# A two-layer conv/RWKV-7 trunk on one core: the mixer loop's steps, tiles and queues rearranged

## The chip, the core and the metric

The kernel runs on one NeuronCore of a Trainium2 chip. The metric is the device time of one execution, in microseconds (us); the median of several executions is compared. The engines are PE (TensorE: matmuls and transposes), DVE (VectorE), ACT (ScalarE), POOL (GpSimd) and SP (SyncE, which here only issues DMAs). Each engine works through its own queue of instructions in order, and an instruction waits at the head of its queue until what it needs is there.

## The reference

Two layers; each is a half-step SwiGLU feed-forward block, a token mixer and a second feed-forward block, each followed by `layer_norm(alpha * x + sublayer(x))`. There are 16 meta tokens and 512 tokens, 528 rows of 1024 features, all float32. The mixer has two branches, whose sum is gated:

```python
def _mixer(x, w_in, ...):
    z = x @ w_in
    glu_a, glu_b, zr, gate_c, gate_r = jnp.split(z, ...)
    yc = _conv_branch(glu_a, glu_b, ...)   # depthwise, 31 taps, layer norm, silu, @ conv_wo
    yr = _rwkv_branch(zr, ...)             # 16 heads of 64
    h = jax.nn.sigmoid(gate_c) * yc + jax.nn.sigmoid(gate_r) * yr
    return h @ w_out

def step(S, inp):                          # the RWKV-7 recurrence, for each token
    r_t, w_t, k_t, v_t, kk_t, a_t = inp
    sa = jnp.einsum("bhvk,bhk->bhv", S, -kk_t)
    S = (S * w_t[:, :, None, :] + sa[..., None] * (kk_t * a_t)[:, :, None, :]
         + v_t[..., None] * k_t[:, :, None, :])
    y = jnp.einsum("bhvk,bhk->bhv", S, r_t)
    return S, y
```

The heads' outputs are normalised per head, a bonus term is added, and the result is multiplied by a gate and by `rwkv_wo`.

## The kernel before

Every float32 matrix is split into a high part (a cast on ACT, line 124 for weights) and a low part (a subtraction on DVE, line 133), and a product is three matmuls of the parts. Rows are worked in two halves of 264 columns. A large product is thus a series of 128x264 matmuls: line 186 in the feed-forward blocks and at the join, line 204 in the mixer loop.

A layer runs as feed-forward, **mixer loop**, **join** (products with `rwkv_wo`, `conv_wo`, `w_out`), feed-forward. The recurrence is done in a chunked form: 8 chunks of 64 tokens and one of the 16 meta tokens, for 4 "quarters" of 4 heads. For a quarter the loop has these steps:

- `prep`: the projections of keys, values and the like (line 204), norms of the keys by a product with a block matrix `bones` (lines 882, 884), a reciprocal root on DVE (lines 339 to 346), transposes of it (line 894), a bonus product (944), elementwise work.
- `scores`: for each chunk, transposes (993) and products (1002) into PSUM tiles `sc`, two copies on ACT (1008), four masks on DVE (1010, 1012), and a write of the result to DRAM (1014).
- `substitution`: the triangular 16x16 blocks of all 32 matrices, read back from DRAM with blocks on partitions (1056), are inverted by 15 pairs of small DVE instructions (1035, 1039). ACT copies the transposed result (1042), SP writes both to DRAM (1059) and loads them in another layout as `dd` (1063). The meta block has a substitution of its own on four partitions.
- `inverse`: the 16x16 inverses are joined to 64x64 ones by short products (1081, 1092) with DVE masks (1083) and ACT copies (1085, 1096).
- `scan`: the chunks in order; each has short products (1167, 1175, 1177, 1184, 1192) and a state update on DVE (1187, 1188). `scores` of the next quarter is emitted along with it at lower priority.
- `post`: group norm per head (lines 1220 to 1241), transposes (1289), bonus and gate (1293, 1294), and a write of the rows to DRAM (1295). For the last quarter these writes are issued by POOL.

Two kinds of work fill the gaps. The convolution has 8 x 30 **taps** on DVE (line 821, each a 128x528 multiply-add into `cacc`), emitted at the lowest priority, the last 15 of a layer behind the last quarter's group norm. On TensorE, 32 **fill units** of 48 matmuls (line 204: the convolution's inputs and the gates) are emitted where the table `FILL` says.

The order on an engine is set by a scheduler, from the order in which the program emits instructions, their priorities and its own model of their times. A tile in a pool with `bufs=1` is written anew only when its last reader is done. At the join the branch's rows come back from DRAM by SP (line 1355), eight tiles in three fetches, are split on ACT and DVE (99, 100), and the first dense matmul (186) reads them.

Of the kernel before, what the change touches and what calls it, by code (L numbers as in the profile page):

```python
# [41 lines left out]
LOTS = (2, 2, 2, 1)  # L42
LOW = [(j, o) for o in range(8) for j in (0, 2)] + [(1, o) for o in range(8)]
NORMB = "ch"
# [5 lines left out]
CLATE = 16  # L50
# [15 lines left out]
BONB = 1  # L66
# [19 lines left out]
class Trunk:  # L86
# [10 lines left out]
    def split(self, x, hi, lo):  # L97

        self.nc.scalar.copy(hi, x)
        self.nc.vector.tensor_tensor(lo, x, hi.bitcast(F32), op=ALU.subtract)  # L100

    def wunit(self, *srcs, dst=None, dma=False):
# [20 lines left out]
        if self.cuts == 1 or not CUTA:  # L123
            self.nc.scalar.copy(hi[:, :kt], raw[:, :kt])  # L124
# [6 lines left out]
        for i in range(0, kt, n):  # L131
            k = slice(i, i + n)
            self.nc.vector.tensor_tensor(lo[:, k], raw[:, k], hi[:, k].bitcast(F32), op=ALU.subtract)  # L133
# [61 lines left out]
    def mac(self, pm, w, x, t0, n, nk, wk=0, xk=0, first=True, last=True):  # L195
# [4 lines left out]
        for k in range(nk):  # L200
            for j, (a, b) in enumerate(((hi, xh), (hi, xl), (lo, xh))):
                for h in range(2):
                    s = t0 + h * n
                    nc.tensor.matmul(  # L204
                        pm[:, h, :n], a[:, wk + k, :], b[:, xk + k, s:s + n],
                        start=first and k == 0 and j == 0,
                        stop=last and k == nk - 1 and j == 2)


    def setup(self):  # L210
# [49 lines left out]
        self.behind = None  # L260

# [72 lines left out]
    def rsqrt(self, x, np_, n):  # L334
# [6 lines left out]
        for _ in range(3):  # L341
            e = nc.vector if NEWTON else nc.gpsimd
            e.tensor_tensor(t, y, y, op=ALU.mult)
            if NEWTON:
                e.scalar_tensor_tensor(t, t, -0.5, x, op0=ALU.mult, op1=ALU.mult)
                e.scalar_tensor_tensor(y, t, 1.5, y, op0=ALU.add, op1=ALU.mult)
            else:
                e.tensor_tensor(t, t, x, op=ALU.mult)
                e.tensor_scalar(t, t, -0.5, 1.5, op0=ALU.mult, op1=ALU.add)
                e.tensor_tensor(y, y, t, op=ALU.mult)  # L350
# [227 lines left out]
    def mixer(self, l, last, pre, more):  # L578
# [28 lines left out]
        mpool, self.mp = self.enter(f"mix{l}")  # L607
        cpool, self.cvp = self.enter(f"conv{l}")
# [896 lines left out]
```

## Time and profile before

| | us |
|---|---|
| median of 3 executions (3315.62 to 3325.91) | 3321.35 |
| the profiled execution's own time | 3312.69 |
| its span in the profile | 3311.0 |
| feed-forward blocks of both layers: 0 to 428, 1262 to 2077, 2902 to 3311 | 1652 |
| mixer loops: 428 to 1118 and 2077 to 2745 | 1358 |
| joins: 1118 to 1262 and 2745 to 2902 | 301 |

The stages' bounds were read off the first and last instructions of their lines in the trace. A row that groups instructions names the line, the engine, the operation, the tile written and the tiles read, the shapes and the count; then the busy time and the mean of one in ns; then how long the engine stood idle just before these instructions, and what it waited for. A row of waits reads "engine, tile and line that waited <- engine, tile and line waited for: us in total, times, longest". A row in order of time has start and length in us; a number in brackets behind it is the idle time just ahead of it on that engine. PE's granted clock is given as a share of full speed.

### The profile page before, as it was taken

Reading aid. Unit: us, or ns where it says so; the run is one execution under the profiler, and the core shown is the slowest. Engines: PE = TensorE matmul, PEld = TensorE weight load, DVE = VectorE, ACT = ScalarE, POOL = GpSimd, SP = SyncE. Lnnn points to the kernel's source line nnn. Section 1 sums busy time; section 2 is a strip of 40 time slices with the busy share of each in tenths; the row PEclk is TensorE's granted clock in tenths of the full one; section 3 lists DMA queues with packets and bytes.
Section 4 is the critical chain, followed back from the end, with each engine's and each line's share of the span. In section 5 each row is a group of like instructions: output and inputs, shape, how many; then the busy total and the mean of one; then the engine's idle time right before and its main releaser. Section 6 shows DMA issues by size and latency. Waiting matters only on the chain.

```text
span 3311.0 us, 64968 instructions
## 1 busy us (share of the span) xinstructions
PE 3154.2 (95%) x27172; PEld 3028.1 (91%) x27172; DVE 1957.2 (59%) x4171; ACT 1228.9 (37%) x2469; POOL 19.7 (1%) x89
## 2 busy tenths in 40 slices
PE   9999999799999899999999999997999998999998
PEld 8999989689889799999989999896898897999997
DVE  4343478787874876343453435697878648663434
ACT  4232254244444444232242322542444444342322
POOL 0000000000000000000000000000000000000000
PEclk9999999798989899999999999997999898999998
DMA  5232244223323552232232322542323235432321
GB/s 153 72 107 78 82 152 131 60 61 102 96 83 97 159 145 81 81 108 83 79 96 75 111 75 74 171 120 53 82 85 98 83 100 163 137 90 79 108 81 52
DMA packets 569012, 326.48 MB, mean 99 GB/s; under 512 B 83148, under 2 KB 535104, under 8 KB 568718
## 3 DMA queue, kind: packets, MB, share of 16 engines
q1 hardware_dynamic: 563726, 312.74, 32.9%
q10 hardware_dynamic: 4608, 8.52, 0.7%
q8 instruction: 213, 3.49, 0.4%
q0 software_dynamic: 384, 1.07, 0.1%
q14 instruction: 81, 0.66, 0.1%
HBM read 270.81 MB, written 47.12 MB: 96 GB/s over the span
## 4 chain that ended last, share of the span: by engine, by line
PE 85%; DVE 8%; ACT 3%; issue 2%; DMA 2%; SPq 0%; ACTq 0%; DVEq 0%
PE mm L186 52%; PE mm L204 18%; PE sc L1002 2%; DVE cacc L821 1%; PE ch L1192 1%; PE sc L1092 1%; PE tr L1167 1%; PE ch L1184 1%; DVE is L1035 1%; DVE ix L1039 1%; PE tr L1175 1%; DVE w_lo L133 1%; PE sc L757 1%; PE ch L1092 1%; PE ch L882 1%
## 5 line engine op out<-in xcount | busy, mean ns | idle before, releaser
L186 PE MATMUL mm<-xh,w_hi 128*128 128x264 f32 (+1 forms) x2880 | 819.5, 286 | 17.0 <-ACT xh L396 16.3
L186 PE MATMUL mm<-xh,w_lo 128*128 128x264 f32 (+1 forms) x2880 | 821.3, 285 | 0.5 <-DVE w_lo L133 0.5
L186 PE MATMUL mm<-xl,w_hi 128*128 128x264 f32 (+1 forms) x2880 | 819.0, 285 | 0.3 <-DVE xl L397 0.2
L133 DVE TENSOR_TENSOR w_lo<-w_raw,w_hi 128x1024 fp32r<-128x1024 f32 (+3 forms) x524 | 528.4, 1011 | 470.1 <-ACT w_hi L124 388.0
L124 ACT CAST w_hi<-w_raw 128x1024 fp32r<-128x1024 f32 (+2 forms) x396 | 380.7, 963 | 788.1 <-PE mm L186 540.0
L186 PEld LDWEIGHTS mm<-xh,w_hi 128*128 128x128 f32 x2880 | 546.0, 190 | 19.7 <-ACT xh L396 17.9
L186 PEld LDWEIGHTS mm<-xh,w_lo 128*128 128x128 f32 x2880 | 547.6, 190 | 0.8 <-DVE w_lo L133 0.8
L186 PEld LDWEIGHTS mm<-xl,w_hi 128*128 128x128 f32 x2880 | 546.9, 190 | 1.0 <-DVE xl L397 0.9
L204 PE MATMUL mm<-xh,w_hi 128*128 128x264 f32 x1760 | 399.1, 304 | 40.0 <-DVE v L705 16.2
L204 PE MATMUL mm<-xh,w_lo 128*128 128x264 f32 x1760 | 394.2, 302 | 15.7 <-DVE w_lo L133 15.7
L186 PE MATMUL mm<-hl,w_hi 128*128 128x264 f32 (+1 forms) x1408 | 400.5, 284 | 0.0
L186 PE MATMUL mm<-hh,w_hi 128*128 128x264 f32 (+1 forms) x1408 | 400.3, 284 | 0.0
L186 PE MATMUL mm<-hh,w_lo 128*128 128x264 f32 (+1 forms) x1408 | 398.7, 283 | 0.0
L204 PE MATMUL mm<-xl,w_hi 128*128 128x264 f32 x1760 | 397.1, 303 | 0.0
L821 DVE SCALAR_TENSOR_TENSOR cacc<-cu,cw,cacc 128x528 f32<-128x528 f32 (+1 forms) x480 | 362.6, 755 | 25.3 <-ACT cacc L819 17.7
L204 PEld LDWEIGHTS mm<-xh,w_hi 128*128 128x128 f32 x1760 | 294.9, 200 | 49.7 <-issue 22.6
L204 PEld LDWEIGHTS mm<-xh,w_lo 128*128 128x128 f32 x1760 | 293.8, 200 | 22.4 <-DVE w_lo L133 16.6
L204 PEld LDWEIGHTS mm<-xl,w_hi 128*128 128x128 f32 x1760 | 294.1, 200 | 6.6
L444 DVE TENSOR_TENSOR g<-g,mm 128x264 f32<-128x264 f32 (+1 forms) x176 | 74.8, 427 | 334.2 <-PE mm L186 321.7
L186 PEld LDWEIGHTS mm<-hh,w_lo 128*128 128x128 f32 x1408 | 265.1, 188 | 0.1
L186 PEld LDWEIGHTS mm<-hl,w_hi 128*128 128x128 f32 x1408 | 264.9, 188 | 0.2
L186 PEld LDWEIGHTS mm<-hh,w_hi 128*128 128x128 f32 x1408 | 264.6, 188 | 0.1
(333 smaller groups left out, 4471.7 us busy)
## 6 DMA issues: line engine op xcount, KB each, us to landing
w_raw<-in_w_in_dram SPq DMA_DIRECT2D x116, 512.0 KB
w_raw<-in_ffn_wg_dram SPq DMA_DIRECT2D x88, 512.0 KB
w_raw<-in_ffn_wu_dram SPq DMA_DIRECT2D x88, 512.0 KB
w_raw<-in_ffn_wd_dram SPq DMA_DIRECT2D x64, 384.0 KB
w_raw<-in_ffn_wd_dram SPq DMA_DIRECT2D x64, 320.0 KB
w_raw<-in_rwkv_wo_dram SPq DMA_DIRECT2D x16, 512.0 KB
w_raw<-in_conv_wo_dram SPq DMA_DIRECT2D x16, 512.0 KB
w_raw<-in_w_out_dram SPq DMA_DIRECT2D x16, 512.0 KB
```

The lines of the kernel that those rows point to most:

```text
L124: self.nc.scalar.copy(hi[:, :kt], raw[:, :kt])
L133: self.nc.vector.tensor_tensor(lo[:, k], raw[:, k], hi[:, k].bitcast(F32), op=ALU.subtract)
L186: self.nc.tensor.matmul(pm, a[:, k, :], b[:, xk + k, s], start=first and k == 0 and j == 0, stop=last and k == nk - 1 and j == 2)
L204: nc.tensor.matmul(pm[:, h, :n], a[:, wk + k, :], b[:, xk + k, s:s + n], start=first and k == 0 and j == 0, stop=last and k == nk - 1 and ...
L444: nc.vector.tensor_tensor(g, g, ps[1][:, :n], op=ALU.mult)
L757: nc.tensor.matmul(pm, w[a][r, o, :], x[b][r, s], start=j == 0, stop=j == 2)
L821: tap = nc.vector.scalar_tensor_tensor(y, x, w, y, op0=ALU.mult, op1=ALU.add)
L882: nc.tensor.matmul(tr[:, 2 * j:2 * j + 2], sq[:, NM + j * P:NM + (j + 1) * P], self.bones[:, ::HS], start=True, stop=True)
L1002: pairs.append(nc.tensor.matmul(ps[e][:, p * P:(p + 1) * P], FB[p][r, fs], G[r, p, 1, :, cs], start=True, stop=True))
L1035: steps.append(nc.vector.tensor_tensor(yv, M[r, j, j + 1:, None].to_broadcast([n, w, k]), X[r, j, None, 0:k].to_broadcast([n, w, k]), op=A ...
L1039: steps.append(nc.vector.tensor_tensor(xv, xv, yv, op=ALU.add))
L1092: nc.tensor.matmul(ps[0:W, i * w:(i + 1) * w], vt[:, i, :], x[:, NM * b0:C], start=True, stop=True)
```

## The change

The computation is the same. The parts are:

- **Taps** are emitted a few at a time at each step of `prep`, `scores` and `scan`, by the tables `TAP0`, `TAPP` and `TAP`, with a priority little below their neighbours' (`TAP_LATE`), and go into two buffers of `cacc`. All are emitted before the loop ends. The first tap after a reciprocal root or a substitution is ordered behind its last step (`self.hold`).
- **Substitution in halves**: each half of a quarter has four chunks' blocks on 64 partitions; the first half takes the meta block's four matrices along (68 partitions), so that these have no substitution of their own. The first half is emitted after half of the score chunks, the second after all. `inverse` runs in halves too; the second is emitted in the first scan step.
- **Masks in one step**: `sc` is one PSUM tile of two banks instead of two tiles of one. A chunk has two masks instead of four and one copy instead of two; the bonus product and the low-rank products are read out in one instruction as well.
- **32 columns**: the last of the short inverse products are 32 columns wide instead of 16, and those with `bones` 32 instead of 2.
- **Fill units** move: two stand at the fourth score chunk and two at the eighth of the first quarter, two and one in later `prep` steps, three in the last scan, and the last one behind the last transposes of the loop (`LAST`, `self.later`).
- **The branch's rows** are fetched by POOL instead of SP. Tiles of the mixer and the join are reserved in a fixed order (`places`), and the first splits of the join's weights are ordered behind the last split of those rows (`self.first`). The scratch space for DMAs that POOL describes is set to 4096 bytes.

Line numbers shift: 204 becomes 214, 821 becomes 872, 894 becomes 940, 1010 and 1012 become 1050 and 1052, 1035 and 1039 become 1077 and 1080, 1042 becomes 1084, 1081 becomes 1112, 1092 becomes 1121, 1289 becomes 1303, 1295 becomes 1309, 1355 becomes 1370.

```diff
-FILL = ((0, 0, 0, 0, 0, 0), 2, (0, 0, 0, 0, 0, 2), (4, 4, 5, 5), ((0, 0, 0, 0, 0, 1), (0, 0, 0, 0, 0, 0)))
-CONV_LATE = 4000
+FILL0 = (0, 0, 0, 0, 2, 0, 0, 0, 2)
+FILL = ((0, 0, 0, 0, 0, 0, 0, 0), (0, 0, 0, 0, 0, 0, 0, 0), (0, 0, 0, 0, 0, 0, 0, 0), (0, 1, 0, 1, 0, 1, 0, 0))
+FILLS = (3, 3, 4, 2)
+LAST = 1
+SCORES = (2, 1, 1, 1, 1, 1, 1, 1)
+TAP_LATE = 150
...
         for c, _ in enumerate(self.scores(0, Q)):
-            if c == META[0]:
-                self.meta_inverse(0, Q)
+            if c == 4:
+                self.substitution(0, 0, Q)
+            filler(FILL0[c])
+            if c:
+                self.taps(TAP0[2])
+        self.substitution(0, 1, Q)
+        self.inverse(0, 0, Q)
         self.meta(0, Q)
-        self.inverse(0, Q)
-        filler(FILL[1])
...
             for c, _ in enumerate(self.scan(q, Q)):
+                if c == 0:
+                    self.inverse(q, 1, Q)
                 with self.tc.high_priority(offset=-SC_LATE):
-                    next(scores, None)
+                    for _ in range(SCORES[c]):
+                        next(scores, None)
+                        done += 1
+                        if done == 5 and q < 3:
+                            self.substitution(q + 1, 0, N)
...
+                filler(FILL[q][c])
+                self.taps(TAP[q][c])
...
+    def taps(self, n):
+        with self.tc.high_priority(offset=-TAP_LATE):
+            while n > 0 and self.convs:
+                if next(self.convs[0], None) is None:
+                    self.convs.pop(0)
+                else:
+                    n -= 1
...
     def sc(self):
-        return self.pp.tile([P, 512], F32, name="sc", bufs=2)
+        return self.pp.tile([P, 2, 512], F32, name="sc", bufs=1)
...
-            for e in range(2):
-                pv = ps[e][:, 0:2 * P].rearrange("a (p f t) -> a p f t", p=2, f=2)
-                nc.scalar.copy(U.rearrange("a (p e) t -> a p e t", e=2)[:, :, e], pv[C:P, :, 0, :])
...
+            nc.vector.tensor_tensor(SB[:, c, :, 0:C].rearrange("a (p e) t -> a e p t", e=2),
+                                    pv[:, :, :, 1, :], mask[:, 1], op=ALU.mult)
...
-            w = C - NM * b0
-            for (U, d, dt, y, vt), ps in zip(groups, bank):
...
+            c0 = min(NM * b0, C - 2 * NM)
+            for i in range(N):
+                x = dt[:, i] if b0 == 1 else y[:, i // 4, i % 4]
+                nc.tensor.matmul(ps[0:W, i, c0:C], vt[:, i, :], x[:, c0:C],
                                  start=True, stop=True)
...
-            load = nc.sync.dma_start(out=h[:, a:b, s], in_=yrv[:, a:b, s])
+            load = nc.gpsimd.dma_start(out=h[:, a:b, s], in_=yrv[:, a:b, s])
```

What the scheduler makes of this is seen in the order on the engines. First DVE in the first quarter, where the substitution of quarter 0 begins (`is`, `ix`: its steps; `cacc`: taps; `sb`, `G <- sc, msk`: masks of score chunks). Before:

```order
L1035 TENSOR_TENSOR is<-im,ix 64x15
L821 SCALAR_TENSOR_TENSOR cacc<-cu_4629,cw,cacc 128x528
L912 TENSOR_TENSOR G<-G,pi 128x16
L914 TENSOR_TENSOR G<-G,pi 128x512
L821 SCALAR_TENSOR_TENSOR cacc<-cu_4629,cw,cacc 128x528
L1035 TENSOR_TENSOR is<-im,ix 64x15
L1039 TENSOR_TENSOR ix<-ix,is 64x15
L821 SCALAR_TENSOR_TENSOR cacc<-cu_4629,cw,cacc 128x528
L1039 TENSOR_TENSOR ix<-ix,is 64x15
L1035 TENSOR_TENSOR is<-im,ix 64x28
```

The same place now:

```order
L1077 TENSOR_TENSOR is<-im,ix 68x15
L872 SCALAR_TENSOR_TENSOR cacc<-cu_4650,cw,cacc 128x528
L1080 TENSOR_TENSOR ix<-ix,is 68x15
L1050 TENSOR_TENSOR sb<-sc,msk 128x2x2x64
L1077 TENSOR_TENSOR is<-im,ix 68x28
L1052 TENSOR_TENSOR G<-sc,msk 64x2x2x64
L1080 TENSOR_TENSOR ix<-ix,is 68x14x2
L846 SCALAR_TENSOR_TENSOR glus<-glus,mm 128x528
L1077 TENSOR_TENSOR is<-im,ix 68x39
L139 TENSOR_TENSOR w_lo<-w_raw,w_hi 128x1024
L1080 TENSOR_TENSOR ix<-ix,is 68x13x3
```

Before, two lots of 64 partitions went through the steps behind all the score chunks; now the first half stands among the masks of the last chunks, and the second follows it.

Then TensorE at the inverse of quarter 0 (`sc`, `tr`, `ch` are PSUM tiles; `mm` the fill). Before:

```order
L204 MATMUL mm<-xh,w_lo 128x264 x2
L1092 MATMUL sc<-dd,b_6300 48x48 x16
L1092 MATMUL tr<-dd,b_6301 48x48 x8
L1092 MATMUL ch<-dd,b_6301 48x48 x8
L1092 MATMUL sc<-G,b_6300 48x32 x16
L1092 MATMUL tr<-G,b_6301 48x32 x8
L1092 MATMUL ch<-G,b_6301 48x32 x8
L1092 MATMUL sc<-G,b_6300 48x16 x16
L1092 MATMUL tr<-G,b_6301 48x16 x8
L1092 MATMUL ch<-G,b_6301 48x16 x8
L1162 MATMUL tr<-ident,v 64x128 x2
```

Now:

```order
L214 MATMUL mm<-xl,w_hi 128x264 x2
L214 MATMUL mm<-xh,w_lo 128x264 x2
L1121 MATMUL sc<-dd,b_6379 48x48 x16
L1150 MATMUL ch<-ut,xt 16x64 x4
L214 MATMUL mm<-xh,w_hi 128x264 x2
L214 MATMUL mm<-xl,w_hi 128x264 x2
L214 MATMUL mm<-xh,w_lo 128x264
L1121 MATMUL sc<-G,b_6379 48x32 x16
L1226 MATMUL ch<-ut 64x64
L1229 MATMUL ch<-ut 64x64
```

A train of 96 short products has become three groups of 16 for a half, with fill and the meta chunk's products between them.

Last, the end of the loop in layer 0, on DVE behind the last group norm (`b <- b, rs` is its last step, `G` the rows being finished, `rl` the low part of the fetched rows). Before:

```order
L1241 TENSOR_TENSOR b_11663<-b_11663,rs_12397 128x512
L821 SCALAR_TENSOR_TENSOR cacc<-cu_4631,cw,cacc 128x528 x2
L1293 TENSOR_TENSOR G<-G 128x256
L821 SCALAR_TENSOR_TENSOR cacc<-cu_4631,cw,cacc 128x528
L1294 TENSOR_TENSOR G<-G 128x256
L1293 TENSOR_TENSOR G<-G 128x256
L821 SCALAR_TENSOR_TENSOR cacc<-cu_4631,cw,cacc 128x528
L1294 TENSOR_TENSOR G<-G 128x256
L821 SCALAR_TENSOR_TENSOR cacc<-cu_4631,cw,cacc 128x528 x7
L133 TENSOR_TENSOR w_lo<-w_raw,w_hi 128x1024 x2
L100 TENSOR_TENSOR rl<-h,rh 128x528 x3
```

Now:

```order
L1262 TENSOR_TENSOR b_11219<-b_11219,rs_12024 128x512
L1307 TENSOR_TENSOR G<-G 128x256
L1308 TENSOR_TENSOR G<-G 128x256
L1307 TENSOR_TENSOR G<-G 128x256
L1308 TENSOR_TENSOR G<-G 128x256
L139 TENSOR_TENSOR w_lo<-w_raw,w_hi 128x1024 x2
L104 TENSOR_TENSOR rl<-h,rh 128x528 x8
```

The taps are gone from here. The fetch (`h <- yscr`) stood in SP's queue behind two weight loads; it stands in POOL's queue now, behind POOL's own writes of the last rows:

```order
L948 MEMSET pi 128x8
L1309 DMA yscr_4415<-G 128x272 x2
L1309 DMA yscr_4415<-G 128x256 x2
L1370 DMA h<-yscr_4415 128x3x528 x2
L1370 DMA h<-yscr_4415 128x2x528
```

More of the change, by code (lines that the diff above doesn't have):

```diff
@@ L65 @@
 JHEAD = 2
-BONB = 1
 SQ = 1
@@ L123, in wunit @@
         if self.cuts == 1 or not CUTA:
-            self.nc.scalar.copy(hi[:, :kt], raw[:, :kt])
+            copy = self.nc.scalar.copy(hi[:, :kt], raw[:, :kt])
+            if self.first is not None:
+                self.nosync(copy, self.first[0])
         if dma:
@@ L653, in mixer @@
                         next(early) if c < G3 + 5 else None
-                if c == META[0] and q < 3:
-                    self.meta_inverse(q + 1, N)
-                if c == META[1] and q < 3:
-                    self.meta(q + 1, N)
-            for _ in scores:
-                pass
+                filler(FILL[q][c])
+                self.taps(TAP[q][c])
             for _ in post:
@@ L662, in mixer @@
             if q < 3:
-                self.inverse(q + 1, N)
+                self.substitution(q + 1, 1, N)
+                self.inverse(q + 1, 0, N)
+                self.meta(q + 1, N)
             post = early or self.post(q, Q)
-            filler(FILL[3][q])
-            Q, N = N, prep(q + 2, FILL[4][q]) if q < 2 else None
+            filler(FILLS[q])
+            Q, N = N, prep(q + 2) if q < 2 else None
         for _ in post:
             pass
-        filler(2 * KT + 2 * KT)
+        filler(len(fill) - LAST)
+        self.later = self.turned
+        filler(len(fill))
+        self.later = None
+        self.taps(KT * TAPS)
         self.cuts = 1
@@ L674, in mixer, with places @@
         return self.mixer_end(more(l + 1))
+    def places(self):
+        tile = lambda name, shape, bufs=1: self.mp.tile([P, *shape], F32, name=name, bufs=bufs)
+        tile("tmp", (T,), TMP)
+        for name in ("kp", "k2", "a", "pinv", "cum"):
+            tile(name, (T,))
+        tile("pi", (1 + NM + NCH * (C + 1),))
+        tile("glus", (T,))
+        tile("sb", (NCH, 4, 2 * C))
+        self.rows()
+        tile("b4", (NCH * 4, 32), B4)
+        tile("ut", (NCH * 4, C))
+        tile("v", (T,), 4)
+        tile("dd", (NCH * 4, C))
+        tile("FB", (2 * T,), 2)
+        for name in ("rx", "rk"):
+            tile(name, (P,))
+        for name in ("im", "ix", "it"):
+            tile(name, (NM, NM), 2)
     def mm(self):
@@ L1040, in substitution @@
         for later, earlier in zip(steps[1:], steps):
             self.nosync(later, earlier)
+        self.hold = steps[-1]
         nc.scalar.copy(XT, X.rearrange("s t i -> s i t"))
-        return X, XT
-    def inverse(self, q, Q):
-        nc, mp = self.nc, self.mp
-        N = NCH * 4
-        G, dd = Q["G"].rearrange("a p e f t -> a (p e) f t"), self.dd
-        blocks = [slice(NM * b, NM * b + NM) for b in range(4)]
-        def load(M):
-            for b, r in enumerate(blocks):
-                nc.sync.dma_start(out=M[b * N:(b + 1) * N], in_=self.ms[q, :, r, r])
-        for f, x in enumerate(self.substitution(P, load, LOTS[q])):
-            nc.sync.dma_start(out=self.xd[q, f], in_=x)
-        for f in range(2):
+        for f, x in enumerate((X, XT)):
+            nc.sync.dma_start(out=self.xd[q, g, f], in_=x[0:4 * N])
```

303 lines of the change are left out of this document (141 added, 162 removed).

## Prediction

> **What bounds the kernel now.** I read the page first, then the busy time by stretches, then who waited for whom, then the order of time at the waits. The page's span, its busy times and its chain of work:
>
> ```profile
> span 3311.0 us, 64968 instructions
> PE 3154.2 (95%) x27172; PEld 3028.1 (91%) x27172; DVE 1957.2 (59%) x4171; ACT 1228.9 (37%) x2469; POOL 19.7 (1%) x89
> PE 85%; DVE 8%; ACT 3%; issue 2%; DMA 2%; SPq 0%; ACTq 0%; DVEq 0%
> 1281.77 364.23 PE mm L186 x2980
> ```
>
> TensorE is the bound. The last row is a piece of the chain inside a feed-forward block: 2980 matmuls in 364.23 us, 122 ns each, without a break. Nothing can be won there by hiding; the change doesn't touch it. So the question is what TensorE loses in the mixer loop. The stretches below (start:end, length; busy us of PE, PEld, DVE, ACT, POOL; granted clock; DMA share, GB/s) are the loop of layer 0, then its first quarter from the second norm to the first state update, one scan (the first updates of quarter 0), the stretches from scan to scan for quarters 1, 2 and 3, and the tail after the last update; then the same in layer 1, without a scan:
>
> ```profile
> 428.00:1118.00 690.00, 637.04 (x5980) 582.53 (x5980) 516.82 (x1341) 295.33 (x706) 6.40 (x32) 0.91 0.36 103
> 533.60:676.70 143.10, 119.75 (x1038) 110.35 (x1036) 115.88 (x298) 48.05 (x113) 1.31 (x10) 0.83 0.31 83
> 676.70:707.90 31.20, 31.09 (x363) 26.07 (x362) 25.22 (x79) 19.06 (x57) 0.44 (x2) 1.00 0.29 79
> 707.90:817.90 110.00, 101.58 (x944) 96.36 (x943) 83.91 (x209) 37.32 (x95) 0.72 (x6) 0.88 0.30 80
> 855.60:955.50 99.90, 94.96 (x882) 89.56 (x881) 81.47 (x205) 38.22 (x98) 0.57 (x4) 0.90 0.33 89
> 995.50:1056.10 60.60, 60.60 (x654) 56.83 (x654) 23.30 (x65) 23.11 (x65) 0.00 (x0) 0.92 0.40 107
> 1089.60:1122.40 32.80, 17.93 (x137) 16.21 (x137) 26.51 (x51) 15.17 (x27) 1.71 (x4) 0.74 0.59 197
> 2182.60:2322.80 140.20, 117.95 (x1022) 108.55 (x1020) 114.87 (x298) 47.27 (x113) 1.31 (x10) 0.84 0.31 83
> 2353.90:2460.10 106.20, 100.29 (x930) 95.62 (x929) 83.22 (x207) 38.07 (x96) 0.72 (x6) 0.89 0.31 82
> 2496.00:2606.30 110.30, 100.16 (x885) 94.00 (x885) 86.06 (x209) 39.19 (x99) 0.58 (x4) 0.86 0.31 82
> 2642.80:2701.50 58.70, 58.70 (x643) 55.12 (x642) 21.88 (x62) 22.29 (x65) 0.00 (x0) 0.94 0.44 115
> 2735.50:2767.70 32.20, 19.36 (x144) 17.50 (x143) 25.95 (x49) 15.13 (x27) 1.07 (x2) 0.73 0.57 189
> ```
>
> A stretch loses two things: the time in which PE is idle (length minus busy), and, of the busy time, the share that the clock withheld. For the first quarter of layer 0 that is 143.1 - 119.75 = 23.4 us idle and 119.75 x 0.17 = 20.4 us of clock. By the same rule:
>
> - first quarters: 43.7 + 41.1 = **84.8 us** (45.6 idle, 39.2 clock)
> - quarters 1, 2, 3: 20.6 + 14.4 + 4.8 and 16.9 + 24.2 + 3.5 = **84.4 us** (29.4 idle, 55.0 clock)
> - tails: 19.5 + 18.1 = **37.6 us** (27.7 idle, 9.9 clock)
>
> 207 us in all, 6% of the span. The scan row shows what is left elsewhere: clock 1.00 and 0.1 us idle. 207 us is the most that better hiding can bring.
>
> Who is late? TensorE's waits in layer 0, and the largest of layer 1:
>
> ```profile
> PE mm L204 <- DVE v L705: 8.8, 1, 8.8
> PE sc L894 <- ACT tmp L892: 7.7, 1, 7.7
> PE mm L204 <- DVE glus L801: 7.2, 1, 7.2
> PE mm L186 <- ACT rh L99: 6.5, 1, 6.5
> PE tr L1289 <- DVE b L1241: 4.3, 1, 4.3
> PE mm L204 <- DVE w_lo L133: 12.7, 3, 7.0
> ```
>
> The fill matmuls (L204, the branch's projections) are late because their weights are split late, and these rows of ACT and SP in the first quarter say why:
>
> ```profile
> 606.26 0.65 ACT L1042 COPY it<-ix 128x256 f32<-128x256 f32 x1 [11.21 <-issue]
> 610.38 1.04 ACT L124 CAST w_hi<-w_raw 128x1024 fp32r<-128x1024 f32 x1 [3.47 <-PE mm L204]
> 606.25 0.34 SPq L1059 DMA_DIRECT2D xdscr<-ix  x1
> 607.98 4.02 SPq L1063 DMA_DIRECT2D dd<-xdscr  x8
> 625.97 2.17 ACT L1085 COPY G<-dd 64x512 f32<-64x512 f32 x4
> ```
>
> ACT sits 11.21 us at the head of its queue with the transposing copy of the substitution (L1042). Behind it stands the next weight cast, and TensorE runs dry. The copy waits for the substitution on DVE, which is itself stretched: its 60 short steps stand among convolution taps of 0.76 us. DVE is busy 115.88 of 143.1 us here.
>
> **Step 1: the first quarter.** DVE's prices are these rows (line, form, count; busy us, mean ns):
>
> ```profile
> L821 DVE SCALAR_TENSOR_TENSOR cacc<-cu,cw,cacc 128x528 f32<-128x528 f32 (+1 forms) x480 | 362.6, 755 | 25.3 <-ACT cacc L819 17.7
> L1035 DVE TENSOR_TENSOR is<-im,ix 64x28 f32<-64x28 f32 (+17 forms) x330 | 64.6, 196 | 7.0
> L1010 DVE TENSOR_TENSOR sb<-sc,msk 128x128 f32<-128x128 f32 x128 | 36.1, 282 | 15.2 <-ACT ut L1008 13.8
> L1012 DVE TENSOR_TENSOR G<-sc,msk 64x128 f32<-64x128 f32 x128 | 35.0, 274 | 0.4
> L945 DVE TENSOR_TENSOR tmp<-v,sc 128x264 f32<-128x264 f32 x32 | 13.6, 426 | 0.6 <-PE sc L944 0.3
> ```
>
> Substitution: a quarter had 60 steps in two lots plus 30 for the meta block, 90 x 0.196 = 17.6 us; now two halves of 30, the meta block riding in the first, 60 x 0.196 = 11.8 us: 6 us less. Masks: a chunk had 2 x 282 + 2 x 274 = 1112 ns, now two of twice the size; the nearest row of that size (L945, 264 elements out of PSUM) is 426 ns, so 852 ns, 2 us less for eight chunks. Taps between the second norm and the first update are as many as before. DVE thus carries 115.9 - 8 = 108 us.
>
> TensorE's own work at full clock was 119.75 x 0.83 = 99.4 us, and two more fill units (48 matmuls of 122 ns each, 5.9 us) are placed ahead of the first scan: 111 us. So both engines come within some 3% of each other, and what was lost to waits can only go if their order fits. It fits better in two places. The first half is substituted after four chunks, beside the four others and their fill, so that its copy and the round trip through DRAM (606.25 to past 612.0 for issue alone, first use of dd on ACT at 625.97) run while TensorE still has scores to make. And 109 fill matmuls, 13.3 us, stand between the last score product and the first inverse product. A half's 30 steps with ten taps between (6 + 8 us) and the round trip (4 us of issue and the time to land, some 10 in all) are about 24 us; two fill units and those 109 matmuls alone are 25, and four chunks of scores come on top. What stays: the L894 transposes behind DVE's reciprocal root (7.7 us, and taps still stand near it). I leave one such wait and its half clock, 8 + 6 = 14 us a layer. Gain 84.8 - 28 = **57 us**. Bounds: all of it goes (85), or DVE, at 97% of TensorE's time, keeps half of the idle and the clock all of its loss (23).
>
> **Step 2: quarters 1 to 3.** Idle 29.4 us: the same blocked cast (the w_lo row of layer 1 and the glus row above). The first half's substitution now lies in the scan before, the second half's has only 30 steps to hold up the cast, about 7 us without taps. I leave a quarter of the idle, 7 us. Clock: 55.0 us. This is how it falls, in quarter 1 of layer 0:
>
> ```profile
> 768.60:771.60 3.00, 3.00 (x68) 3.00 (x69) 1.44 (x2) 1.71 (x9) 0.00 (x0) 1.00 0.22 84
> 774.50:779.60 5.10, 5.10 (x66) 5.06 (x64) 0.00 (x0) 1.71 (x6) 0.00 (x0) 0.50 0.00 0
> 779.60:788.00 8.40, 8.40 (x40) 8.40 (x40) 5.50 (x15) 1.67 (x3) 0.00 (x0) 0.50 0.22 64
> ```
>
> The clock is 1.00 at the start of the inverse's short products (68 in 3.0 us, 44 ns each), 0.50 by their end, and stays so for 8.4 us of full-sized fill. PE counts as busy throughout, so it is not an idle gap alone that lowers it; 96 short products stand in one train there. In the new order they come 16 at a time with fill between. I take it that half of the clock loss goes, 27 us left: the trains are cut, but norms, scores and scans of short products remain. Columns: 16 became 32 in the last of these products; in the first row above products of 48 and of 32 columns pass at the same 44 ns, so 0. Gain 84.4 - 34 = **50 us**; bounds 15 (idle halved, clock as it is) and 84.
>
> The Trainium skill ("TensorE: Matmul & The Clock Gate", Part 1: The HAM clock gate) has it that the clock halves after one idle window of about 3.4 us and comes back after one busy window of as much. By it 8.4 us of busy half clock cannot be, and the waits alone would carry the clock: with every wait gone the 104 us of clock loss would go too, the first rival below. The rows above speak against it; no idle gap precedes 774.5.
>
> **Step 3: the tail.** After the last update, layer 0:
>
> ```profile
> 1104.95 0.41 PE L1289 MATMUL tr<-ident,b 128*128 128x128 f32 x2 [4.34 <-DVE b L1241]
> 1105.68 0.90 SPq L1355 DMA_DIRECT2D h<-yscr  x2
> 1108.90 5.59 DVE L821 SCALAR_TENSOR_TENSOR cacc<-cu,cw,cacc 128x528 f32<-128x528 f32 x7
> 1109.28 0.54 POOL L1295 DMA_DIRECT2D yscr<-G  x1 [0.81 <-DVE G L1294]
> 1111.43 1.70 ACT L99 CAST rh<-h 128x528 fp32r<-128x528 f32 x3 [1.52 <-DMA h<-yscr]
> ```
>
> The taps leave DVE (seven stand in one block ahead of the splits). 59 fill matmuls, 7.2 us, now stand ahead of the last transposes where 27 stood (3.3 us, then 4.34 idle): that gap closes. 55 more, 6.7 us, stand behind them. But the fetch goes to POOL's queue behind its own four row writes. The last of those was issued 4.3 us after the transposes began (1109.28 - 1104.95), the fetch took 5.75 us (1105.68 to 1111.43), and the first split takes about 1 (the last row's 1.70 are for three casts): 11 us against 6.7 of fill. I leave 5 us idle and 2 of clock a layer: gain 37.6 - 14 = **24 us**; bounds 10 and 37.
>
> **The rest.** Reserved memory and the order of the join's splits lie beside 140 us of dense matmuls: 0. The halves add DMAs to SP (dd loads 8 to 16 a quarter; 8 took 4.02 us to issue), and weight loads queue behind them; they are prefetched: 0, at worst 4 us for each of eight halves.
>
> **Sum.** 57 + 50 + 24 = 131 us. The profiled execution took 3312.69 us (span 3311.0); the median is 3321.35, 8.7 above. 3321.35 - 131 = **3190 us**. All lower bounds together give 48 us, 3273; all upper ones 206, 3115; the forecast's own range is half-way to each, 3152 to 3232.
>
> **Rivals.**
> - *Full clock:* if idle gaps or long trains are all that lowers the clock, it stays at 1.00, and the waits go but for the tails' 10 us: 207 - 10 = 197, 3125 us. For it: scans of short products run at 1.00. Against: the half-clock row at 100% busy. 0.14.
> - *The clock stays as lost:* trains cut, but it falls all the same. Then 104 us of clock remain instead of the 12 + 27 + 4 = 43 that I leave in steps 1 to 3: 61 less is won, 3251 us. 0.11.
> - *New waits in the scan:* sc was two tiles of one bank, now one of two. Each score chunk in a scan holds it from its first transpose to the second mask; the next chunk's transposes wait at the head of TensorE's queue with the scan behind them. 48 chunks in both layers at 1.3 us each: 62 us back, 3253 us. Against: scores stand a chunk per scan step, and DVE is idle 6 of 31.2 us there. 0.08.
> - *Slower:* the same wait, where taps of 0.76 us stand ahead of the masks. Above 131 / 48 = 2.7 us a chunk (three taps and two masks) it decides; at 3.3 us it costs 158: 3348 us. 0.07.
> - *The order moves the waits and hides none:* DVE at 97% beside TensorE; the blocked cast merely waits for another half: 3321 us. 0.05.
>
> **How the numbers follow.** My forecast has 0.55. 3110 to 3275 takes in all but the last two rivals and the ends of the bounds (about 0.15 left out). A measurement of this kernel tells 0.3%, 10 us, from no change. Faster: 0.55 + 0.14 + 0.11 + 0.08 = 0.88; same 0.05; slower 0.07.
>
> **What would show it.** First quarter: 143 us plus 12 of fill becomes 125; ACT's wait at the substitution's copy below 4 us; DVE above 85% busy there. Scan to scan: clock above 0.94, no half-clock rows behind the inverse. Scan: 31.2 us and clock 1.00 but for moved fill; waits of score transposes for masks would show the third rival. Tail: no gap ahead of the last transposes, one of about 5 us ahead of the join. I am wrong if waits for w_lo at fill matmuls stay near 7 us, or if the clock in the loop stays at 0.91.

## The result, and the profile after

| | before | changed |
|---|---|---|
| median, us | 3321.51 (3315.62 to 3325.91, 4 executions) | 3210.31 (3199.37 to 3214.85, 4 executions) |
| ratio | | 0.9661, 95% interval 0.9632 to 0.9691 |
| span of the profiled execution | 3311.0 | 3211.3 |

The change makes the kernel 111 us faster; 3190 was forecast, in a range of 3110 to 3275. The page of the changed kernel, its span, busy times and chain:

```profile
span 3211.3 us, 64489 instructions
PE 3129.7 (97%) x27172; PEld 3006.6 (94%) x27172; DVE 1893.0 (59%) x3827; ACT 1224.3 (38%) x2271; POOL 24.0 (1%) x95
PE 89%; DVE 5%; ACT 3%; DMA 2%; issue 1%; SPq 0%; ACTq 0%; POOL 0%; POOLq 0%; DVEq 0%
```

TensorE's busy time fell by only 25 us, its idle time by 75. Stretches of the changed kernel, as before the change (start:end, length; busy us of PE, PEld, DVE, ACT, POOL; granted clock; DMA share, GB/s). In layer 0: first quarter, to quarter 1's first update, the rest of quarter 1's scan, to quarter 2's, to quarter 3's; in layer 1: first quarter, the stretches to quarters 1, 2 and 3:

```profile
532.90:649.40 116.50, 114.28 (x1002) 107.57 (x1001) 104.69 (x245) 45.85 (x86) 1.30 (x10) 0.96 0.37 101
689.60:778.60 89.00, 86.35 (x785) 81.03 (x784) 74.28 (x193) 37.95 (x80) 1.17 (x8) 0.92 0.38 102
778.60:830.60 52.00, 49.31 (x490) 40.60 (x490) 34.37 (x87) 21.61 (x56) 0.00 (x0) 0.77 0.18 49
830.60:908.20 77.60, 77.47 (x700) 73.04 (x700) 61.13 (x166) 32.63 (x70) 1.02 (x6) 0.91 0.40 105
953.20:998.10 44.90, 44.90 (x443) 40.72 (x442) 33.55 (x90) 15.86 (x38) 0.00 (x0) 0.86 0.46 126
2136.70:2260.50 123.80, 119.86 (x970) 112.75 (x969) 101.84 (x242) 46.05 (x85) 1.30 (x10) 0.89 0.37 96
2301.00:2385.80 84.80, 84.77 (x775) 79.94 (x775) 73.41 (x191) 37.35 (x78) 1.16 (x8) 0.94 0.39 103
2430.10:2497.70 67.60, 67.52 (x638) 63.60 (x637) 55.98 (x162) 30.91 (x66) 1.02 (x6) 0.95 0.37 97
2546.60:2589.30 42.70, 42.70 (x430) 38.84 (x429) 31.67 (x81) 15.69 (x37) 0.00 (x0) 0.88 0.42 111
```

Length minus PE busy is now 2.2 us in the first quarter of layer 0 where it was 23.4, and 0 to 2.7 us between the scans. The clock column is what is left: 0.86 to 0.95 between the scans, 0.96 and 0.89 in the first quarters, and 0.77 in one scan that ran at 1.00 before.

I split the whole span of each profiled execution in three: PE **idle**; **clock**, half of the time in which PE was busy at half clock; and **work**, the rest, which is what PE would need at full clock. Before: 156.8 + 105.4 + 3048.7. Changed: 81.7 + 82.4 + 3047.3. So of the 99.7 us of the two profiled spans, 75 are idle time, 23 clock and 1 work. The medians lie 111 us apart: the profiled execution of before was 9 us under its median, that of the changed kernel 3 us above.

The waits tell the same. TensorE's waits in the changed kernel, in the rows that answer to those of before, ACT, SP and TensorE at the first half's substitution of quarter 0, and last the row of all sixteen transposing copies (busy us, mean ns, then idle time before them):

```profile
PE mm L196 <- ACT rh L103: 8.4, 2, 4.5
PE sc L940 <- ACT tmp L938: 5.0, 3, 2.1
PE tr L1303 <- DVE b L1262: 4.1, 2, 3.7
PE mm L214 <- DVE w_lo L139: 0.3, 1, 0.3
586.90 0.66 ACT L1084 COPY it<-ix 68x256 f32<-68x256 f32 x1
588.72 1.06 ACT L128 CAST w_hi<-w_raw 128x1024 fp32r<-128x1024 f32 x1 [1.16 <-PE mm L214]
589.13 4.07 SPq L1089 DMA_DIRECT2D dd<-xdscr  x8
594.29 2.06 PE L1112 MATMUL sc<-dd,ut 64*64 64x48 f32 x32
598.29 1.03 ACT L1115 COPY G<-dd 64x1024 f32<-64x1024 f32 x1
L1084 ACT COPY it<-ix 68x256 f32<-68x256 f32 (+1 forms) x16 | 10.4, 651 | 22.3 <-DVE ix L1080 22.0
```

No wait is shown ahead of this transposing copy; at all sixteen together ACT still waits 22.3 us, where it was 58.2. The weight cast behind this one waits for TensorE, as the cast behind the copy did before (3.47 us in the prediction's rows). Fill waits for `w_lo` 0.3 us in the whole kernel. Of `dd`, TensorE first uses one part 5 us after the loads are issued (line 1112) and ACT the other after 9 us; TensorE has matmuls in the meantime. Score transposes (line 1034) wait for no mask; no row of waits names them.

What fill waited for before the change is seen at its longest wait, in the first quarter of layer 0 (steps of the substitution on DVE, then `v`, which DVE reads out of a PSUM tile `mm`, then TensorE; last the row of these waits in both layers):

```profile
598.46 0.45 DVE L1035 TENSOR_TENSOR is<-im,ix 64x55 f32<-64x55 f32 x2
598.94 0.45 DVE L1039 TENSOR_TENSOR ix<-ix,is 64x55 f32<-64x55 f32 x2
601.26 0.18 DVE L1035 TENSOR_TENSOR is<-im,ix 64x28 f32<-64x28 f32 x1
601.48 0.77 DVE L705 SCALAR_TENSOR_TENSOR v<-mm,omtm,e 128x528 f32<-128x528 f32 x1
602.39 0.78 PE L204 MATMUL mm<-xh,w_hi 128*128 128x264 f32 x2 [8.78 <-DVE v L705]
PE mm L204 <- DVE v L705: 16.2, 2, 8.8
```

TensorE waits for `v`, and `v` stands in DVE's own queue behind the steps, with no tap among those of the last 8 us. TensorE runs again at 602.39, while ACT stands at its copy until 606.26. Six waits of fill before the change, the five longest among them, are of this kind (8.8, 7.4, 7.2, 7.0, 5.4 and 3.0 us, 39 in all, for `v`, `glus` and `w_lo`): DVE had no idle time to speak of ahead of what was waited for, and 11 to 33 steps passed during each wait. The changed kernel has none of them.

### The profile page after: what moved, and what is told of

Same layout as the page of the kernel before. It is cut to its first block, busy times and chain, and to the rows that moved or that the text cites. A ratio compares the mean times of both kernels' runs of the same rounds, so it can differ in the third digit from the quotient of the medians.

```text
span 3211.3 us, 64489 instructions
## 1 busy us (share of the span) xinstructions
PE 3129.7 (97%) x27172; PEld 3006.6 (94%) x27172; DVE 1893.0 (59%) x3827; ACT 1224.3 (38%) x2271; POOL 24.0 (1%) x95
## 4 chain that ended last, share of the span: by engine, by line
PE 89%; DVE 5%; ACT 3%; DMA 2%; issue 1%; SPq 0%; ACTq 0%; POOL 0%; POOLq 0%; DVEq 0%
PE mm L196 54%; PE mm L214 19%; PE sc L1121 3%; PE sc L1043 1%; PE tr L1188 1%; PE ch L1213 1%; PE tr L1196 1%; PE ch L1205 1%; PE sc L1112 1%; PE sc L928 1%; PE sc L797 1%; PE tr L1183 1%; DVE w_lo L139 1%; DVE ln_rstd L390 1%; PE sc L1034 1%
## 5 line engine op out<-in xcount | busy, mean ns | idle before, releaser
L196 PEld LDWEIGHTS mm<-xh,w_lo 128*128 128x128 f32 x2880 | 546.3, 190 | 0.8 <-DVE w_lo L139 0.8
L196 PEld LDWEIGHTS mm<-xl,w_hi 128*128 128x128 f32 x2880 | 545.6, 189 | 1.4 <-DVE xl L405 1.3
L214 PE MATMUL mm<-xl,w_hi 128*128 128x264 f32 x1760 | 386.4, 297 | 0.0
L872 DVE SCALAR_TENSOR_TENSOR cacc<-cu,cw,cacc 128x528 f32<-128x528 f32 (+1 forms) x480 | 355.1, 751 | 5.9 <-ACT cacc L870 2.7
L214 PEld LDWEIGHTS mm<-xh,w_lo 128*128 128x128 f32 x1760 | 286.6, 195 | 7.3 <-DVE w_lo L139 0.7
L214 PEld LDWEIGHTS mm<-xl,w_hi 128*128 128x128 f32 x1760 | 285.5, 195 | 6.3
```

The source lines that it names most:

```text
L196: self.nc.tensor.matmul(pm, a[:, k, :], b[:, xk + k, s], start=first and k == 0 and j == 0, stop=last and k == nk - 1 and j == 2)
L214: m = nc.tensor.matmul(pm[:, h, :n], a[:, wk + k, :], b[:, xk + k, s:s + n], start=first and k == 0 and j == 0, stop=last and k == nk - 1 ...
L872: tap = nc.vector.scalar_tensor_tensor(y, x, w, y, op0=ALU.mult, op1=ALU.add)
```

## The experiments

Times are medians. In each profiled execution idle, clock and work are taken as above; "changed" and "before" stand for the two kernels.

| run | us | ratio to before, interval | idle | clock | work |
|---|---|---|---|---|---|
| before | 3321.5 | | 156.8 | 105.4 | 3048.7 |
| changed | 3210.3 | 0.9661 (0.9632 to 0.9691) | 81.7 | 82.4 | 3047.3 |
| e1: 64 columns | 3182.2 | 0.9585 (0.9557 to 0.9612) | 76.6 | 23.0 | 3070.6 |
| e2: 16 and 2 columns | 3230.8 | 0.9729 (0.9701 to 0.9756) | 82.5 | 91.6 | 3049.0 |
| e3: taps low | 3198.6 | 0.9634 (0.9615 to 0.9652) | 75.0 | 67.2 | 3052.1 |
| e4: first half late | 3232.2 | 0.9730 (0.9706 to 0.9755) | 88.6 | 89.6 | 3050.1 |
| e5: 48 columns | 3163.1 | 0.9532 (0.9503 to 0.9562) | 73.4 | 30.0 | 3053.3 |
| e6: one piece | 3261.6 | 0.9813 (0.9782 to 0.9843) | 110.4 | 109.1 | 3039.9 |
| e7: before, 64 columns | 3296.7 | 0.9925 (0.9904 to 0.9946) | 153.5 | 74.9 | 3067.7 |
| e8: before, few taps | 3260.6 | 0.9815 (0.9793 to 0.9837) | 110.7 | 87.9 | 3051.5 |
| e9: 48 columns, taps low | 3161.4 | 0.9516 (0.9502 to 0.9530) | 72.7 | 29.4 | 3057.8 |
| e10: fetch by SP | 3211.4 | 0.9664 (0.9642 to 0.9685) | 86.8 | 76.3 | 3045.9 |
| e11: fill behind | 3215.1 | 0.9682 (0.9660 to 0.9705) | 85.4 | 72.6 | 3049.4 |

The scheduler lays an edited kernel out anew, so instructions beside the edit shift too. Executions of one kernel spread over 6 to 22 us, and the clock term of a single profile with them (e1's profile is of its fastest execution); differences under some 10 us are not read.

**e1, 64 columns.** The clock was what the change left, and it still fell with PE fully busy.

```diff
-            nc.tensor.matmul(ps[0:C, i, 0:W], U[:, i, :], d[:, i, 0:W], start=True, stop=True)
+            nc.tensor.matmul(ps[0:C, i, :], U[:, i, :], d[:, i, :], start=True, stop=True)
...
-            c0 = min(NM * b0, C - 2 * NM)
+            c0 = 0
```

> The changed kernel with all short products of the inverse 64 columns wide (lines 1112 and 1121; 48 and 32 before). Theory A (the clock falls because products of few columns leave the array idle between them although PE counts as busy): the half-clock stretches behind the first-half inverses go, the clock loss in the loops falls from 68 us to 35 or less, and the time from 3210 to 3175-3190 us. Theory B (short products in themselves lower the clock, whatever their columns): the same stretches remain, 3205-3220 us. If wider products cost issue time: 1024 more columns per half at most, slower than 3215.

3182 us: theory A. The same place in the changed kernel and in e1, at the inverse of quarter 1's first half: two groups of L1121 products with fill between; then what stands ahead of the last group; then this group and what follows, 9 us. The changed kernel:

```profile
722.90:727.40 4.50, 4.50 (x79) 4.12 (x77) 1.66 (x9) 1.89 (x5) 0.00 (x0) 1.00 0.50 153
727.40:730.60 3.20, 3.20 (x37) 2.78 (x34) 1.97 (x5) 1.83 (x5) 0.00 (x0) 0.82 0.00 0
730.60:739.60 9.00, 9.00 (x63) 8.74 (x63) 4.22 (x19) 1.25 (x4) 0.00 (x0) 0.50 0.01 2
```

And e1:

```profile
720.60:725.80 5.20, 5.14 (x77) 4.77 (x77) 4.89 (x19) 2.71 (x6) 0.00 (x0) 1.00 0.79 240
725.80:727.70 1.90, 1.90 (x23) 1.67 (x21) 1.70 (x6) 0.63 (x2) 0.00 (x0) 1.00 0.16 45
727.70:736.70 9.00, 9.00 (x99) 8.81 (x99) 6.44 (x20) 3.10 (x6) 0.42 (x2) 1.00 0.23 31
```

PE is busy without a gap in the changed kernel, and but for 0.06 us in e1. With wide products the clock stays at 1.00, and 99 matmuls pass in 9 us where 63 did (the mix behind the group differs somewhat). The changed kernel has eight half-clock stretches of this sort, one in each quarter of both layers: each begins behind 3.4 us in which PE was 100% busy, mostly with the first half's L1121 products, and they hold 44 of its 82 us of clock. In e1 two of them are left, with 5 us. The price is work: 3047.3 to 3070.6, 23 us. It is the products' own time. A window on one group of L1121 products in each kernel (32 columns in the changed one, then 64 in e1, then 48 in e5):

```profile
602.00:603.40 1.40, 1.40 (x33) 1.40 (x32) 1.14 (x6) 0.00 (x0) 0.00 (x0) 1.00 0.73 225
604.40:606.20 1.80, 1.80 (x33) 1.78 (x32) 1.63 (x7) 0.82 (x2) 0.00 (x0) 1.00 0.04 14
602.60:604.00 1.40, 1.40 (x33) 1.40 (x32) 1.19 (x7) 0.00 (x0) 0.00 (x0) 1.00 0.72 228
```

A group of 16 products is 32 records, two for each product. A record takes about 44 ns with 32 or 48 columns, 56 with 64.

**e2, columns as before.** The reverse: `c0 = NM * b0`, and the norm's products of 2 columns.

```diff
-            c0 = min(NM * b0, C - 2 * NM)
+            c0 = NM * b0
...
-            nc.tensor.matmul(tr[:, 32 * j:32 * j + 32], sq[:, k0:k0 + P], self.bones[:, ::4],
+            nc.tensor.matmul(tr[:, 2 * j:2 * j + 2], sq[:, k0:k0 + P], self.bones[:, ::HS],
```

> The changed kernel with the columns of before: 16 in the last inverse products, 2 in the norm's (line 928). Theory A: more or longer half-clock stretches behind inverses and norms, clock loss 80 us or more, time 3220-3240 us. Theory B (columns do not matter): 3205-3215 us.

3231 us, 20 more, with idle and work unchanged: the "32 columns" of the change, in the inverse and in the norm together, are worth some 20 us. The two profiles are 12 us apart, 9 of them clock; the mean granted clock is 0.964 to 0.971 in the executions of e2 and 0.970 to 0.975 in those of the changed kernel.

**e5, 48 columns** only for L1121 (`c0 = NM`), between the 32 that cost clock and the 64 that cost time.

> The changed kernel with all short products of the inverse 48 columns wide (line 1121: 48 in place of 32; line 1112 is 48 already). With 64 columns TensorE's work at full clock grew by 23 us and the clock loss fell by 59. If a product's time grows with its columns only beyond what its issue covers, and if the clock needs columns in proportion: work grows by under 10 us, the clock loss falls by 30 to 55 us, time 3165-3190 us. If only full 64 columns hold the clock: the stretches behind the inverses remain, 3205-3220 us.

3163 us, the first case (2 us under its range): clock 30, work only 6 above the changed kernel. Of the eight stretches behind L1121 two are left here too. This version beats both kernels.

**e7, 64 columns in the kernel before.** Lines 1081 and 1092:

```diff
-                nc.tensor.matmul(ps[0:C, i * W:(i + 1) * W], U[:, i, :], d[:, i, 0:W],
+                nc.tensor.matmul(ps[0:C, i * C:(i + 1) * C], U[:, i, :], d[:, i, :],
...
-                    nc.tensor.matmul(ps[0:W, i * w:(i + 1) * w], vt[:, i, :], x[:, NM * b0:C],
+                    nc.tensor.matmul(ps[0:W, i * C:(i + 1) * C], vt[:, i, :], x,
```

> The kernel before with the short products of the inverse (lines 1081, 1092) 64 columns wide. If few columns lower the clock there too: no half-clock stretch begins within a train of L1092 any more, the clock loss falls from 105 to 50-75 us, the work grows by 23, the idle of 157 us stays: 3280-3310 us. If in that kernel the clock falls because of the idle gaps: loss stays near 105, 3320-3345 us.

3297 us: clock 105.4 to 74.9, work up 19, idle unchanged. Columns lower the clock loss there too; of the 26 half-clock stretches that stay, 17 begin behind 3.4 us in which PE was idle for more than half of the time. One part of the expectation fell: three stretches still begin at these trains, with PE busy 73, 81 and 98% of the 3.4 us before. Four more begin behind fully busy windows that hold short products of the meta chunk.

**e3, taps at the lowest priority.**

```diff
-TAP_LATE = 150
+TAP_LATE = 4000
```

> The changed kernel with the taps at the lowest priority again (offset 4000 instead of 150). If the placement of the taps removed the waits: fill matmuls wait for w_lo or for DVE again by 20 us or more, ACT waits at the substitution's copy (line 1084) by over 40 us, taps stand at the loops' ends, time 3240-3290 us. If the halves alone removed them: 3205-3220 us.

3199 us, below both cases: the taps' higher priority brings nothing here. The steps at which they are emitted, the order behind a substitution (`self.hold`) and the second buffer are as in the changed kernel, so these are not tested. The waits for `w_lo` do not come back. Only the last transposes wait longer, as the row of e3's waits says:

```profile
PE tr L1303 <- DVE b L1262: 9.1, 2, 5.2
```

The 12 us by which it is faster lie in the main in the clock (82 to 67), and e9 shows no such gain on top of 48 columns.

**e9, both.**

> 48 columns (run e5, 3163 us) and the taps at the lowest priority (run e3, 3199 us against 3210). If the two add: 3145-3158 us. If the taps' placement is worth nothing and e3 gained by a half-clock stretch that happened not to come: 3158-3170 us, like e5.

3161 us, within e5's interval: the second case.

**e4, the first half late.** It is substituted behind all score chunks.

```diff
         for c, _ in enumerate(self.scores(0, Q)):
-            if c == 4:
-                self.substitution(0, 0, Q)
...
+        self.substitution(0, 0, Q)
         self.substitution(0, 1, Q)
...
-                        if done == 5 and q < 3:
+                        if done == 9 and q < 3:
```

> The changed kernel with the first half's substitution emitted only behind all score chunks of its quarter. If starting it among the scores is what hides its copy and the round trip: TensorE waits at the inverse or at fill by 3 us or more in most of the eight places, time 3230-3260 us. If there is fill enough behind the scores for both halves: 3205-3220 us.

3232 us, as the first case had it, but by another way: the waits at the inverse are small (2.5 us for `dd` in all), and the 22 us are spread over 7 us of idle and 7 of clock in the profile.

**e6, one piece.** Both halves go through the steps in lockstep, behind all chunks.

```diff
+        for j in range(NM - 1):
+            w, k = NM - 1 - j, j + 1
+            todo = []
+            for np_, M, X, XT in lots:
+                ...
+                todo.append((x, y))
+            for x, y in todo:
+                steps.append(nc.vector.tensor_tensor(x, x, y, op=ALU.add))
```

> The changed kernel with both halves' substitution in lockstep behind all score chunks, as before the change (the steps of the two halves alternate, 60 short steps in place of 30 ahead of the first copy); the inverse stays in halves. If the halving is what removed the idle: over the late half of run e4 (3232 us) TensorE's idle grows by another 20 us or more, 3250-3290 us. If the fill and masks removed it: within 10 us of e4, 3222-3242 us.

3262 us: 29 more than e4 and 51 more than the changed kernel, with 29 us of idle and 27 of clock over the latter. But the waits of before do not come back with it. The copies in e6, steps of both lots on DVE, and waits of TensorE:

```profile
L1087 ACT COPY it<-ix 68x256 f32<-68x256 f32 (+1 forms) x16 | 10.0, 642 | 4.4 <-DVE ix L1082 4.3
595.72 0.34 DVE L1077 TENSOR_TENSOR is<-im,ix 68x55 f32<-68x55 f32 x2
595.97 0.33 DVE L1082 TENSOR_TENSOR ix<-ix,is 68x55 f32<-68x55 f32 x2
PE mm L214 <- DVE v L743: 4.5, 2, 2.3
PE tr L1199 <- ACT w L1193: 5.0, 9, 1.1
PE tr L1306 <- DVE b L1265: 14.6, 2, 7.5
```

ACT waits 4.4 us at the copies, less than in the changed kernel, and TensorE 4.5 us for `v`, where it was 16.2. Nor is this quite the piece of before: there both lots lay in one tile, and two steps of 55 elements took 0.48 us from start to start; here each lot has its own tile, and they take 0.25. So e6 prices a late single piece at 51 us, but not by way of the copy. The last transposes wait 10 us more than in the changed kernel and those of the scan (line 1199) 4.5 more; how this comes of the substitution is open.

**e8, few taps in the kernel before.** Two of each 31 taps are left in; the convolution branch is not computed.

```diff
-        for j in range(TAPS):
+        for j in (0, TAPS - CLATE):
```

> The kernel before with 2 of each 31 convolution taps left in (the output of the convolution branch is not computed). If the taps stretch the substitution and so block ACT: its wait at the copy (line 1042, 40 us in three places of the page) falls below 10 us and TensorE's idle of 157 us to 100 or less, 3220-3270 us. If the wait comes from the dependent steps and DRAM alone: idle 140 us or more, 3295-3325 us.

3261 us in time, but neither case in mechanism. Idle falls by 46 us; the copy's wait hardly falls. Its row (busy, mean ns, idle before it) in e8, and in e4, where the taps are all there but the halves are separate:

```profile
L1042 ACT COPY it<-ix 4x256 f32<-4x256 f32 (+1 forms) x16 | 10.2, 636 | 50.0 <-issue 29.2 <-DVE ix L1039 20.8
```

```profile
L1083 ACT COPY it<-ix 68x256 f32<-68x256 f32 (+1 forms) x16 | 10.4, 647 | 28.6 <-DVE ix L1079 27.8 <-DVE cu L620 0.7
```

It was 58.2 us before the change. With few taps 50.0 remain: the taps are not the main cause of this wait. With halves it is 28.6 in e4 and 22.3 in the changed kernel, in waits of 6.4 us at most. What the taps cost lay elsewhere: with few of them TensorE's waits for `v` fall from 16.2 to 5.1 us and those for `tmp` (line 892) from 16.2 to none, while those of fill for `w_lo` only fall from 15.7 to 12.8.

**e10, fetch by SP.**

```diff
-            load = nc.gpsimd.dma_start(out=h[:, a:b, s], in_=yrv[:, a:b, s])
+            load = nc.sync.dma_start(out=h[:, a:b, s], in_=yrv[:, a:b, s])
```

> The changed kernel with the fetch of the branch's rows in SP's queue again. If POOL's queue, behind its own writes, delays the fetch: TensorE's waits for rh at the join (4.5 and 3.9 us) shrink, 3200-3208 us. If SP's queue with its weight loads is the slower: they grow to 6 us or more, 3212-3222 us. If the rows' own round trip sets it: within 3 us of 3210.

In the waits it is the second case, in the time the third: 3211 us. TensorE's wait in e10, and the fetch of layer 0 there, then the fetch in the changed kernel:

```profile
PE mm L196 <- ACT rh L103: 18.5, 2, 9.3
1048.90 11.55 SPq L117 DMA_DIRECT2D w_raw<-in_rwkv_wo_dram  x3
1060.50 1.21 SPq L1370 DMA_DIRECT2D h<-yscr  x2
1066.60 1.70 ACT L103 CAST rh<-h 128x528 fp32r<-128x528 f32 x3 [5.32 <-DMA h<-yscr]
1053.65 0.54 POOL L1309 DMA_DIRECT2D yscr<-G  x1 [0.26 <-DVE G L1308]
```

```profile
1061.06 0.54 POOL L1309 DMA_DIRECT2D yscr<-G  x1 [0.25 <-DVE G L1308]
1061.93 1.51 POOL L1370 DMA_DIRECT2D h<-yscr  x2 [0.33 <-issue]
1069.18 1.70 ACT L103 CAST rh<-h 128x528 fp32r<-128x528 f32 x3 [0.48 <-DMA h<-yscr]
```

On SP the fetch stands behind three weight loads that hold the queue for 11.55 us; the last row write went out at 1053.65 (its row stands last), and the fetch 6.9 us later. On POOL it follows its write by 0.9 us. The wait is 10 us shorter with POOL, but the profile of e10 happened to lose 6 us less to the clock, and no difference in time can be told.

**e11, fill behind.** The four units among the first quarter's score chunks stand behind the meta chunk.

```diff
-FILL0 = (0, 0, 0, 0, 2, 0, 0, 0, 2)
+FILL0 = (0, 0, 0, 0, 0, 0, 0, 0, 0)
...
+        filler(4)
         N = prep(1)
```

> The changed kernel with the four fill units among the first quarter's score chunks moved behind the meta chunk, ahead of the second quarter's preparation. If fill among the scores is what covers the first half's substitution: TensorE waits at the first inverse or at score products in both layers, 5 us or more each with half clock behind it, 3225-3250 us. If the other fill suffices: 3205-3218 us.

3215 us: the second case. The other fill is enough.

## Why the prediction was right, and where its mechanism and its size were off

- **What bounds it**: right. Work is the same before and after (3048.7 and 3047.3); all of the gain is idle and clock, and nothing came from the feed-forward blocks.
- **Idle**: forecast to fall by 70 us in the loops and tails (102.7 by the prediction's rows, 33 left: 8 + 8 in the first quarters, 7 between the scans, 5 + 5 in the tails). It fell by 77 there and by 75 in the whole span. In the first quarters 2.2 and 3.9 us stayed where 8 each were left, in the stretches between the scans 2.9 in all, in the tails 4.9 and 7.6 where 5 each were left.
- **The blocked cast**: wrong as the mechanism. Step 1 has ACT stand at the copy, the weight cast wait behind it, and TensorE run dry for that. The rows of before show TensorE held by `v` in DVE's queue behind the steps of the substitution: it ran again at 602.39, with ACT still at the copy, and the cast behind the copy then waited 3.47 us for TensorE. The 39 us of this kind all went, so the idle came out as forecast, but for another reason than the one given. Which part of the change removed these waits is not shown: with taps at the lowest priority (e3) and with the first half late (e4) there are none either, and with one piece (e6) 4.5 us. That the taps stretch the substitution was the other half of step 1. In the kernel before most of them cost 46 us of idle (e8), but in the main by other waits, and their priority in the changed kernel is worth nothing (e3).
- **Early first half and fill among the scores**: the early start is worth 22 us (e4), though no single wait shows it. The fill units among the scores are not needed (e11): the prediction counted two of them into its 25 us of cover, and what stands behind the scores was enough.
- **The clock is the term that was mis-sized.** Step 2 took it that "half of the clock loss goes", because the trains of short products are cut, and priced the columns at 0. In the loops and tails the prediction left 43 us of clock. The trace has 70 there: 19 in the first quarters (12 forecast), 33 between the scans and 12 in them (27 forecast), 4 in the tails (4 forecast), and 2 ahead of the first quarters. The loss before was sized too high as well: busy time multiplied by the share that the clock withheld in a stretch gave 104 us, but part of the half clock fell on idle time, above all in the first quarters and tails, and while PE worked the same stretches lost 92 (94 with the rest of the loops). So the clock was to give 61 us and gave 24.
- **What decides the clock** is in the main not the train but the columns of its products: e1 leaves the train's order and loses 23 us to the clock in the whole kernel in place of 82. And the price of 0 for 16 to 32 columns was right for a product's time (no more work in the changed kernel than in e2) and wrong for the clock, where they are worth some 20 us (e2).
- **The sum** was 131 us, and the two profiles differ by 100. That 3210 lies only 20 us above 3190 is in part luck: idle fell by 7 us more than forecast, and the medians lie 11 us further apart than the profiled executions.
- **The tail**: right. The gap behind the last group norm closed in layer 0 (3.7 us stayed in layer 1), and waits of 4.5 and 3.9 us stand ahead of the join, where 5 were forecast. Step 3 put the fetch behind POOL's own writes; it follows the last of them by 0.9 us. What it did not price is SP's queue, on which the waits are 9.3 us (e10).
- **Rivals**: new waits in the scan did not come; TensorE's idle time in the eight scans is 4 us, where it was 1. "Full clock" did not come either, but e1 and e5 show that most of it was to be had. "The clock stays as lost" came nearer than the forecast: 70 of 94 us stayed.
- **Its own signs**: the waits for `w_lo` went and the clock of layer 0's loop rose from 0.91 to 0.94. A clock above 0.94 from scan to scan and no half clock behind the inverse were named too, and did not come.

The Trainium skill ("TensorE: Matmul & The Clock Gate", Part 1: The HAM clock gate) has the clock follow how busy PE has lately been, and halve after an idle window of about 3.4 us. Read with PE's busy time, this trace disagrees: the clock falls behind 100% busy windows. Read as the array's own time it would agree: products of 32 and of 48 columns take the same time, so the narrower ones would leave the array idle for longer within each slot, and the clock tells the two apart. No run here shows the array's own time, so this reading is not shown.

What stays open: how much masks in one step, moved fill, low-rank read-outs and the ordering of the joins' splits each bring. Taking back the early halves (51 us, e6) and the 32 columns (20 us, e2) cost the most of the parts that were taken out of the changed kernel; whether they add up was not tried, and the other parts weren't tried apart. The half-clock stretch in the scan of quarter 1 (0.77 in the windows above) starts where short scan products stand with small waits and no fill between; it came in some profiles and not in others, and its trigger wasn't isolated.

## What to carry to other kernels

When TensorE waits for another engine's result, look at what stands ahead of that result in that engine's own queue: here it was a long chain of small steps on DVE (39 us in six waits), and not the copy at which ACT sat idle. A busy TensorE is not yet one that keeps its clock: where many small products run, widen them up to the point at which their time starts to grow (48 columns here, of the 16, 32, 48 and 64 tried), even if the extra columns are thrown away. And a load that something waits for doesn't belong behind prefetches in the same queue.

## What the runs showed of the hardware

- The half-clock stretches in all these traces last 3.41 us or a multiple of it (6.83, 10.24, up to 34.13), but for the last of each execution.
- Eight of them in the changed kernel begin behind 3.4 us in which PE was 100% busy; some of these last 13.65 us with PE busy throughout.
- 48 columns in place of 32 cost nothing per record and cut the clock loss from 82 to 30 us; 64 cost 12 ns more per record and left 23, which single profiles can't tell from 30. The widest product was not the best one.
- Two small DVE steps took 0.48 us from start to start where the two lots that they work on lay in one tile (598.46 to 598.94, before), and 0.25 where each had its own (595.72 to 595.97, e6). What makes the difference was not tried.
- In the one place shown, a DMA that POOL issued took 7.25 us from issue to the cast that used it (1061.93 to 1069.18), one that SP issued 6.1 (1060.50 to 1066.60). The wait behind the slower one was still the shorter, since its queue was free.
